# Softmax reciprocals in a windowed attention: spread over a head's 64 partitions by a trip through DRAM instead of by TensorE

## The chip, the cores and the metric

The kernel runs on one core of a Trainium2 chip. The metric is the time of one execution on the device in microseconds (us). Three runs of the kernel before gave 1763.22, 1763.94 and 2857.5 us; their median, 1763.94 us, is what a change is measured against. One more execution was profiled, and the rows of the profile come from that one.

## What is computed

Two layers act on a latent stream of 1024 tokens and a context prefix of 256 tokens, both 1024 wide. Layer 0 is the gated, windowed, grouped-query attention that this document is about; layer 1 is a bidirectional state-space mixer that takes most of the time and is not touched. The part of the reference that matters here:

```python
def sink_softmax(scores, sink_kg, mask):
    if mask is not None:
        scores = jnp.where(mask, scores, -jnp.inf)
    sink_col = jnp.broadcast_to(sink_kg.astype(jnp.float32)[None, :, :, None, None],
                                scores.shape[:-1] + (1,))
    p = jax.nn.softmax(jnp.concatenate([scores, sink_col], axis=-1), axis=-1)
    return p[..., :-1]
...
        s = jnp.einsum('bqkgd,bskd->bkgqs', qb, kb).astype(jnp.float32) * scale
...
        p = sink_softmax(s, sink_kg, mask).astype(vb.dtype)
        return jnp.einsum('bkgqs,bskd->bqkgd', p, vb)
...
    y_lat = ((o * jax.nn.silu(g)) @ w_out).astype(h_lat.dtype)
```

There are 16 query heads of 64 dimensions, 4 to each of 4 key heads. Latent queries, in blocks of 128, see at most three neighbouring blocks of keys and the two blocks of the context; context queries see the two blocks of the context alone.

## The kernel before, in words

**Units.** The attention runs over 40 units, each a block `b` of 128 queries and a key head `j` with its four query heads. Units 1 to 8 are the two context blocks (two key blocks each), units 9 to 24 the first four latent blocks, units 25 to 40 the last four (four or five key blocks each). A unit has a front and a back. `attention` calls the front of unit x+1 and then the back of unit x (`AHEAD=1`).

**Front (`att_front`, lines 747 to 792).** GpSimd starts the loads of the queries (`qs` at line 757, `qz` at 762), SyncE the load of the gate `sg` (758, tag `sgt`, two buffers). For each of the four heads TensorE forms the scores with queries on the partitions (776, 777), VectorE adds the mask and takes the negative row maximum `nm` (781), ScalarE takes the exponential and accumulates the row sum (783). Then, for the four heads at once: GpSimd adds the sink (786), ScalarE takes its exponential (787), GpSimd adds it to the sums (788), and VectorE takes the reciprocal `sums` (790), 128 queries by 4 heads. GpSimd copies it out to `rs` (791), each value repeated 64 times: 128 queries by 2 by 2 by 64, in one buffer.

**Back (`att_back`, lines 794 to 825).** For each key block TensorE turns the four heads' exponentials (802) into a bank of PSUM named `pt` (two buffers), ScalarE and VectorE split them into a high and a low part (806, 807), and TensorE multiplies both with the values (808, 809) into `pv`, which then holds a head's 64 dimensions on partitions and queries along the row. The sums, though, have queries on partitions. So TensorE turns `rs` with two more transposes into `pt` (815): out come 128 partitions, 64 for each of two heads, with a query's reciprocal in every one of them. VectorE multiplies the gate by them (816). ScalarE copies the lower half of `pv` (818), VectorE adds the two halves (821), GpSimd multiplies the result `ot` with the gate (822), and ScalarE and GpSimd split that for the output projection (824, 825).

**Work beside it.** Between key blocks `tick` issues steps of matrix multiplications that have nothing to do with the unit: projections of queries and gates of the second latent half beside units 1 to 24, output projections beside units 25 to 40 (lines 240 to 242). Their weights come through SyncE (233), are split on ScalarE (223) and GpSimd (225), and are asked for one projection ahead. SyncE also loads and stores the residual stream (863, 868, 893) and stores projected queries and gates (663, 664, 672).

**Order.** The program gives dependencies and priorities, and a scheduler puts each engine's instructions in one fixed order by its own model of time. On the chip each engine, and each queue that starts transfers, then runs its own list in order, waiting on semaphores: what stands behind a waiting instruction waits too. SyncE's list holds nearly all the transfers; GpSimd's list holds its arithmetic and the loads of `qs` and `qz`.

Of the kernel before, what the change touches and what calls it, by code (L numbers as in the profile page):

```python
# [9 lines left out]
F32 = mybir.dt.float32  # L10
# [7 lines left out]
P = 128  # L18
# [11 lines left out]
HD = 64  # L30
# [12 lines left out]
    pj=1, S=2, pt=2, pv=1,  # L43
    rope_b=2, qf=3, qh=3, ql=2, kHH=2, kLL=2, qs=2, sgt=2, sm=8, mx=2, nm=2, es=2, sums=2, ph=2, pl=2, co=1, ot=2,
    oraw=3, h1=3, h1k=8, wada=6, gq=1, sqa=1,
    cacc=2, cctx=1, bT=2, cT=2, xn4=4, xn2=1, bn4=4, bn2=1, sz=2, xw=2, hf=2, hx=2, M=2, bw=2, y2=1, xs=1, uT=2, pj2=2, psX=3, sk=2, dg=2,
)
G0 = 4
AHEAD = 1
# [65 lines left out]
class Kernel:  # L115
# [13 lines left out]
    def t(self, pool, shape, dt, tag, bufs=None):  # L129
        self.n += 1  # L130
        kw = {"bufs": bufs or BUFS.get(tag, 1)}
        return pool.tile(shape, dt, tag=tag, name=f"{tag}_{self.n}", **kw)
# [616 lines left out]
    def att_front(self, p, x, i, j, b):  # L749
        nc, t = self.nc, self.t  # L750
        ps = self.psA
        o = b * P - TT[i][0]
        sg = t(self.psm, [P, 2, P], F32, "sgt")
        nm = t(p, [P, R], F32, "nm")
        sums = t(p, [P, R], F32, "sums")
        qs = t(p, [P, R, P], F32R, "qs")
        nc.gpsimd.dma_start(qs, self.q_d[j][i][:, :, :, o : o + P].rearrange("e s d n -> (s d) e n"))
        nc.sync.dma_start(sg, self.sg_d[j][i][:, :, o : o + P].rearrange("e p n -> p e n"))

        z = j % 2  # L760
        qz = self.qz[z]
        nc.gpsimd.dma_start(qz[z * HD : (z + 1) * HD], self.q_d[j][i][:, z, :, o : o + P].rearrange("e d n -> d e n"))
        if b < 8:
            k0, k1 = max(b - 1, 0), min(b + 2, 8)
        else:
            k0, k1 = 8, 8
        kb = list(range(k0, k1)) + [8, 9]
        c0_ = 512 - (k1 - k0) * P
        m0 = {0: 128, 7: 640}.get(b, 0 if b < 8 else 384)
        W = len(kb) * P  # L770
        sms = []
        for r in range(R):
            S = t(self.psS, [P, 1024], F32, "S")
            for x, (qq, kk) in enumerate(((qs[:, r, :], self.kHH[j]), (qz[:, r, :], self.kL[j // 2]))):
                if k1 > k0:
                    nc.tensor.matmul(S[:, c0_:512], qq, kk[:, k0 * P : k1 * P], start=x == 0, stop=x == 1)  # L776
                scored = nc.tensor.matmul(S[:, 512:768], qq, kk[:, LAT : LAT + CTX], start=x == 0, stop=x == 1)  # L777
            self.scored.append(scored.ins)
            Sv = S[:, c0_:768]
            sm = t(self.psm, [P, 640], F32, "sm")  # L780
            nc.vector.tensor_tensor_reduce(out=sm[:, :W], in0=Sv, in1=self.mask[:, m0 : m0 + W], scale=-SCALE, scalar=self.nsink[:, 4 * j + r : 4 * j + r + 1],  # L781
                                           op0=ALU.add, op1=ALU.min, accum_out=nm[:, r : r + 1])
            nc.scalar.activation(sm[:, :W], sm[:, :W], AF.Exp, bias=nm[:, r : r + 1], scale=-1.0, accum_out=sums[:, r : r + 1])  # L783
            sms.append(sm)
        es = t(p, [P, R], F32, "es")
        nc.gpsimd.tensor_tensor(es, nm, self.sink[:, 4 * j : 4 * j + 4], op=ALU.add)
        nc.scalar.activation(es, es, AF.Exp)
        nc.gpsimd.tensor_tensor(sums, sums, es, op=ALU.add)
        rs = t(self.pb, [P, 2, 2, HD], F32, "rs")
        nc.vector.reciprocal(sums, sums)  # L790
        nc.gpsimd.tensor_copy(rs, sums.rearrange("p (x e) -> p e x", e=2).unsqueeze(3).broadcast_to([P, 2, 2, HD]))
        return j, b, i, o, kb, sms, sg, rs

    def att_back(self, p, st, oH, oL, tick):
        nc, t = self.nc, self.t
        ps = self.psA
        j, b, i, o, kb, sms, sg, rs = st
        pv = t(ps, [P, 512], F32, "pv")
        for x, bb in enumerate(kb):
            pt = t(ps, [P, R, P], F32, "pt")  # L800
            for r in range(R):
                nc.tensor.transpose(pt[:, r, :], sms[r][:, x * P : (x + 1) * P], self.ident)  # L802
            ph = t(self.pb, [P, R * P], F32R, "ph")
            pl = t(self.pb, [P, R * P], F32R, "pl")
            ptf = pt.rearrange("p r n -> p (r n)")
            nc.scalar.copy(ph, ptf)  # L806
            nc.vector.tensor_sub(pl, ptf, ph)  # L807
            nc.tensor.matmul(pv, self.v[:, bb, j, :], ph, start=x == 0, stop=False)  # L808
            mm = nc.tensor.matmul(pv, self.v[:, bb, j, :], pl, start=False, stop=x == len(kb) - 1)  # L809
            self.last.append(mm.ins)  # L810
            tick()

        pt = t(ps, [P, 512], F32, "pt")
        for e in range(2):
            nc.tensor.transpose(pt[:, e * P : (e + 1) * P], rs[:, e].rearrange("p x d -> p (x d)"), self.ident)
        nc.vector.tensor_mul(sg, sg, pt[:, : 2 * P].rearrange("p (a n) -> p a n", a=2))
        co = t(self.pb, [HD, 512], F32, "co")
        nc.scalar.copy(co, pv[HD:, :])
        ot = t(self.pb, [P, 2, P], F32, "ot")
        for e in range(2):  # L820
            nc.vector.tensor_add(ot[e * HD : (e + 1) * HD].rearrange("p a n -> p (a n)"), pv[:HD, e * 256 : (e + 1) * 256], co[:, e * 256 : (e + 1) * 256])
        nc.gpsimd.tensor_tensor(ot, ot, sg, op=ALU.mult)
        oh = oH[i][:, 2 * j : 2 * j + 2, o : o + P]
        nc.scalar.copy(oh, ot)
        nc.gpsimd.tensor_tensor(oL[i][:, 2 * j : 2 * j + 2, o : o + P], ot, oh, op=ALU.subtract)  # L825
# [1039 lines left out]
```

## Time and profile before

| what | value |
|---|---|
| runs | 1763.22, 1763.94, 2857.5 us, median 1763.94 |
| the profiled execution | 1765.51 us, of which 1763.5 us from first to last instruction |
| granted TensorE clock in it | 0.997 |
| attention's units, from the first reciprocal to the last turning of `rs` | 254.8 to 681.8 us |
| TensorE turnings of `rs` (line 815) | 80, two for each unit |
| GpSimd copies to `rs` (line 791) | 40 |

In the rows below, PE is TensorE's matrix multiplication and PEld its load of the stationary operand, which runs beside it; DVE is VectorE, ACT ScalarE, POOL GpSimd and SP SyncE. A row such as "PE L815 MATMUL pt<-ident,rs" names the engine, the line, the operation, what is written and what is read; "x80" counts instructions. Three numbers with slashes are the least, middle and greatest duration in ns. "A <- B: 33.1, 20, 3.2" says that A's engine sat idle before A until B was done, for 33.1 us in 20 cases, 3.2 us at most. For a DMA the last number is the median from its start to its landing. Matrix multiplications are pipelined, so that one row's duration overlaps the next row's; the distance from one start to the next says what one occupies.

### The profile page before, as it was taken

The page shows a single profiled execution, that of the slowest core. Times are in us where ns is not written, and L with a number is a line of the kernel's source. Part 1 is how long each engine was busy: PE and PEld are TensorE (multiplying, and loading weights), DVE is VectorE, ACT ScalarE, POOL GpSimd, SP SyncE. Part 2 cuts the span into 40 slices and gives each one's busy share as a digit, 9 for nine tenths or more (in the row PEclk, how much of TensorE's full clock was granted, in tenths as well). Part 3 has the DMA queues.
Part 4 walks back from the last instruction along what each step waited for, and adds up shares of the span by engine and source line. Part 5 has one row for each costly group of instructions (what it writes and reads, how often), then busy time and mean ns, then how long its engine had stood idle before and what let it go on. Part 6 is the DMA issues. An engine that isn't in the chain of part 4 may idle for free.

```text
span 1763.5 us, 28925 instructions
## 1 busy us (share of the span) xinstructions
PE 1731.7 (98%) x10277; PEld 1498.1 (85%) x10277; DVE 1195.1 (68%) x2115; ACT 872.8 (49%) x1905; POOL 794.1 (45%) x1064
## 2 busy tenths in 40 slices
PE   8999999999999998999999999999999999999997
PEld 6897788888888786889898998989889898988886
DVE  5744436788877876685876867677685867876734
ACT  4522247777777774363544434344443444544522
POOL 3231037555565555104454554636455363554311
PEclk9999999999999999999999999999999999999999
DMA  9468876444564436222223232332332332555533
GB/s 364 169 190 261 277 190 146 102 110 96 118 161 130 120 101 219 75 66 68 77 78 97 73 93 70 87 79 75 91 82 76 89 81 79 179 169 172 176 96 131
DMA packets 211389, 225.52 MB, mean 128 GB/s; under 512 B 15789, under 2 KB 149037, under 8 KB 211245
## 3 DMA queue, kind: packets, MB, share of 16 engines
q1 hardware_dynamic: 177180, 205.02, 38.7%
q0 software_dynamic: 34064, 18.65, 5.9%
q8 instruction: 81, 1.33, 0.3%
q14 instruction: 64, 0.52, 0.1%
HBM read 188.78 MB, written 35.13 MB: 127 GB/s over the span
## 4 chain that ended last, share of the span: by engine, by line
PE 88%; DVE 5%; DMA 3%; issue 2%; ACT 1%; POOL 1%; SPq 0%; DVEq 0%; POOLq 0%; ACTq 0%
PE pj L1243 19%; PE pj L1277 10%; PE pj L1682 7%; PE pj L240 7%; PE pj L242 6%; PE pj L241 6%; PE psD L1227 4%; PE pt L802 3%; PE psX L1430 3%; PE psD L1346 2%; PE pv L809 2%; PE pv L808 2%; PE S L776 2%; PE S L777 2%; PE psX L1399 2%
## 5 line engine op out<-in xcount | busy, mean ns | idle before, releaser
L240 PE MATMUL pj<-uH,wh 128*128 128x512 f32 (+1 forms) x632 | 234.3, 371 | 4.9 <-ACT wh L223 1.7
L242 PE MATMUL pj<-uH,wl 128*128 128x512 f32 (+1 forms) x632 | 222.5, 352 | 1.1 <-POOL wl L225 1.1
L241 PE MATMUL pj<-uL,wh 128*128 128x512 f32 (+1 forms) x632 | 222.2, 352 | 0.4 <-POOL uL L825 0.4
L1321 POOL TENSOR_TENSOR xw<-xn,dtdec 128x256 f32<-128x256 f32 x144 | 95.5, 664 | 212.2 <-PE psD L1346 73.4
L1243 PE MATMUL pj<-uH,wh 128*128 128x512 f32 x512 | 173.3, 410 | 0.0
L1243 PE MATMUL pj<-uH,wl 128*128 128x512 f32 x512 | 170.4, 403 | 0.0
L1243 PE MATMUL pj<-uL,wh 128*128 128x512 f32 x512 | 168.8, 403 | 0.0
L1277 PE MATMUL pj<-wl,uH 128*128 128x256 f32 x512 | 151.0, 295 | 0.0
L1277 PE MATMUL pj<-wh,uH 128*128 128x256 f32 x512 | 150.4, 294 | 0.0
L1277 PE MATMUL pj<-wh,uL 128*128 128x256 f32 x512 | 150.0, 293 | 0.0
L807 DVE TENSOR_TENSOR pl<-pt,ph 128x512 fp32r<-128x512 f32 x168 | 115.0, 689 | 47.5 <-ACT ph L806 46.0
L240 PEld LDWEIGHTS pj<-uH,wh 128*128 128x128 f32 x632 | 119.8, 190 | 23.9 <-issue 3.6
L242 PEld LDWEIGHTS pj<-uH,wl 128*128 128x128 f32 x632 | 119.6, 189 | 20.0 <-POOL wl L225 1.6
L781 DVE CUSTOM_DVE_ANT_0 sm<-S,mask,nsink 128x640 f32<-128x640 f32 (+2 forms) x160 | 119.0, 774 | 24.0 <-PE S L777 18.2
L225 POOL TENSOR_TENSOR wl<-wr,wh 128x512 fp32r<-128x512 f32 x74 | 97.1, 1316 | 79.2 <-ACT wh L223 75.8
L1462 ACT ACTIVATE uT<-psX,nw 128x128 f32<-128x128 f32 x128 | 46.5, 363 | 171.8 <-PE psX L1461 167.7
L241 PEld LDWEIGHTS pj<-uL,wh 128*128 128x128 f32 x632 | 120.0, 190 | 12.3 <-issue 0.8
L783 ACT ACTIVATE sm<-sm,nm 128x640 f32<-128x640 f32 (+2 forms) x160 | 118.5, 743 | 21.5 <-DVE nm L781 20.7
L806 ACT CAST ph<-pt 128x512 fp32r<-128x512 f32 x168 | 97.9, 584 | 48.7 <-PE pt L802 45.5
L223 ACT CAST wh<-wr 128x512 fp32r<-128x512 f32 (+1 forms) x116 | 74.8, 648 | 84.6 <-PE pj L241 59.7
L1243 PEld LDWEIGHTS pj<-uH,wl 128*128 128x128 f32 x512 | 95.9, 188 | 19.9
L1243 PEld LDWEIGHTS pj<-uL,wh 128*128 128x128 f32 x512 | 95.3, 188 | 19.1
(357 smaller groups left out, 4933.0 us busy)
## 6 DMA issues: line engine op xcount, KB each, us to landing
wr<-w_x SPq DMA_DIRECT2D x32, 512.0 KB, 4.2
M<-acs SPq DMA_DIRECT2D x64, 256.0 KB, 5.0
bw<-acs SPq DMA_DIRECT2D x64, 256.0 KB, 5.4
wr<-w_sk SPq DMA_DIRECT2D x24, 512.0 KB, 3.9
wr<-wg SPq DMA_DIRECT2D x40, 256.0 KB, 5.2
qs<-q POOLq DMA_DIRECT2D x40, 256.0 KB, 3.9
wada<-w_ada SPq DMA_DIRECT2D x16, 512.0 KB, 8.0
wr<-wq SPq DMA_DIRECT2D x32, 256.0 KB, 3.4
```

The lines of the kernel that those rows point to most:

```text
L225: (eng or nc.vector).tensor_tensor(l, raw, h, op=ALU.subtract)
L240: self.nc.tensor.matmul(ps, lh, rh, start=first and i == 0, stop=False)
L241: self.nc.tensor.matmul(ps, lh, rl, start=False, stop=False)
L242: self.last_mm = self.nc.tensor.matmul(ps, ll, rh, start=False, stop=last and i == n - 1)
L781: nc.vector.tensor_tensor_reduce(out=sm[:, :W], in0=Sv, in1=self.mask[:, m0 : m0 + W], scale=-SCALE, scalar=self.nsink[:, 4 * j + r : 4 * ...
L783: nc.scalar.activation(sm[:, :W], sm[:, :W], AF.Exp, bias=nm[:, r : r + 1], scale=-1.0, accum_out=sums[:, r : r + 1])
L806: nc.scalar.copy(ph, ptf)
L807: nc.vector.tensor_sub(pl, ptf, ph)
L1243: self.pe = nc.tensor.matmul(raw[:, 512 * i : 512 * i + 512], l[:, k, :], r[i][:, k, :], start=k + y == 0, stop=k == KT - 1 and y == 2)
L1277: self.pe = nc.tensor.matmul(pj[:, c], l, r[:, k, :], start=c % 2 + q + k + y == 0, stop=c % 2 == 1 and q == 1 and k == 3 and y == 2)
L1321: nc.gpsimd.tensor_tensor(xw, X(st, c).rearrange("p (r h) -> p r h", r=R), self.dtdec[:, c, hd(d, g)].unsqueeze(2).broadcast_to([P, R, HP] ...
L1682: self.pe = nc.tensor.matmul(banks[x], l[:, z, sl], r, start=k == 2 * qs[0] and y == 0, stop=k == 2 * qs[-1] + 1 and y == 2)
```

## The change

The reciprocals no longer go through GpSimd and TensorE. At the end of the front SyncE stores `sums` to DRAM, turned around on the way, so that a head's 128 reciprocals lie in a row; the tensor there is a separate one for each unit. At the start of the back SyncE loads them in two transfers, one for each half of the partitions, and reads each row 64 times over, so that the reciprocals arrive as line 816 needs them. The SBUF tile `rs` now has two buffers, each as large as the old one. The two transposes, their use of a `pt` bank and the GpSimd copy are gone; VectorE's multiplication reads SBUF where it read PSUM.

```diff
-        rs = t(self.pb, [P, 2, 2, HD], F32, "rs")
         nc.vector.reciprocal(sums, sums)
-        nc.gpsimd.tensor_copy(rs, sums.rearrange("p (x e) -> p e x", e=2).unsqueeze(3).broadcast_to([P, 2, 2, HD]))
+        rs = t(self.dr, [2, 2, P], F32, f"rs{j}_{b}")
+        nc.sync.dma_start(rs.rearrange("x e q -> q (x e)"), sums)
         return j, b, i, o, kb, sms, sg, rs
...
         pv = t(ps, [P, 512], F32, "pv")
+        rb = t(self.pb, [P, 2, P], F32, "rs")
+        for x in range(2):
+            nc.sync.dma_start(rb[x * HD : (x + 1) * HD], rs[x].unsqueeze(0).broadcast_to([HD, 2, P]))
...
-        pt = t(ps, [P, 512], F32, "pt")
-        for e in range(2):
-            nc.tensor.transpose(pt[:, e * P : (e + 1) * P], rs[:, e].rearrange("p x d -> p (x d)"), self.ident)
-        nc.vector.tensor_mul(sg, sg, pt[:, : 2 * P].rearrange("p (a n) -> p a n", a=2))
+        nc.vector.tensor_mul(sg, sg, rb)
```

The table of buffer counts gets one more entry, `rs=2`.

More of the change, by code (lines that the diff above doesn't have):

```diff
@@ L45 @@
     oraw=3, h1=3, h1k=8, wada=6, gq=1, sqa=1,
-    cacc=2, cctx=1, bT=2, cT=2, xn4=4, xn2=1, bn4=4, bn2=1, sz=2, xw=2, hf=2, hx=2, M=2, bw=2, y2=1, xs=1, uT=2, pj2=2, psX=3, sk=2, dg=2,
+    cacc=2, cctx=1, bT=2, cT=2, xn4=4, xn2=1, bn4=4, bn2=1, sz=2, xw=2, hf=2, hx=2, M=2, bw=2, y2=1, xs=1, uT=2, pj2=2, psX=3, sk=2, dg=2, rs=2,
 )
```

## The prediction, on record before the result

> **What bounds the kernel now.** I read the page's busy times and its chain first, then the stages of the attention, then who waits for whom in them.
>
> ```profile
> span 1763.5 us, 28925 instructions
> PE 1731.7 (98%) x10277; PEld 1498.1 (85%) x10277; DVE 1195.1 (68%) x2115; ACT 872.8 (49%) x1905; POOL 794.1 (45%) x1064
> ...
> PE 88%; DVE 5%; DMA 3%; issue 2%; ACT 1%; POOL 1%; SPq 0%; DVEq 0%; POOLq 0%; ACTq 0%
> ```
>
> TensorE is busy 98% of the span and makes 88% of the chain that ended last; GpSimd makes 1% of it. The change touches only the attention, so I look at its stages (columns: busy us of PE, PEld, DVE, ACT, POOL, then the granted clock, the DMA share and GB/s).
>
> ```profile
> 254.00:300.00 46.00, 44.97 (x247) 37.44 (x248) 30.86 (x99) 34.79 (x101) 32.69 (x54) 1.00 0.66 147
> 300.00:480.00 180.00, 177.39 (x1032) 151.41 (x1031) 145.40 (x319) 132.77 (x297) 101.64 (x152) 1.00 0.48 111
> 480.00:545.00 65.00, 62.68 (x447) 57.20 (x446) 47.70 (x101) 49.22 (x107) 44.48 (x59) 1.00 0.58 153
> 545.00:662.00 117.00, 114.43 (x650) 94.61 (x649) 90.56 (x192) 84.04 (x189) 60.81 (x88) 1.00 0.43 112
> ```
>
> In each stage TensorE has 96 to 99%; VectorE comes next (145.40 of 180, 81%), GpSimd is at 52 to 71%. So TensorE's own work is what a change here is worth, and the other engines matter through the stalls that they give it. Those are, from 250 to 690 us, with the two waits around the removed instructions:
>
> ```profile
> POOL rs L791 <- PE pt L815: 33.1, 20, 3.2
> DVE sgt L816 <- PE pt L815: 5.1, 5, 1.5
> PEld pv L809 <- DVE pl L807: 11.3, 25, 1.0
> PEld pj L241 <- POOL uL L825: 0.8, 1, 0.8
> PEld S L242 <- POOL wl L225: 0.6, 1, 0.6
> ```
>
> GpSimd stands 33.1 us until an earlier unit's turnings free the single `rs`, but TensorE loses only 0.8 and 0.6 us to GpSimd's products. The long wait is on an engine with time to spare.
>
> **What is removed.** The three groups:
>
> ```profile
> L815 PE MATMUL pt<-ident,rs x80: 270/272/328, 259.0 to 681.9; 128*128 128x128 f32 x80
> L791 POOL COPY rs<-sums x40: 389/397/627, 256.4 to 662.3; 128x256 f32<-128x256 f32 x40
> L816 DVE TENSOR_TENSOR sgt<-sgt,pt x40: 407/414/422, 259.5 to 682.3; 128x256 f32<-128x256 f32 x40
> ```
>
> 80 times 272 ns would be 21.8 us, but matmuls overlap, so I take what a pair occupies from the starts of its neighbours:
>
> ```profile
> 414.35 0.40 PE L809 MATMUL pv<-pl,v 128*128 128x512 f32 x1
> 414.58 0.38 PE L815 MATMUL pt<-ident,rs 128*128 128x128 f32 x2
> 414.72 0.49 PE L240 MATMUL pj<-uH,wh 128*128 128x512 f32 x1
> 415.04 0.39 PE L241 MATMUL pj<-uL,wh 128*128 128x512 f32 x1
> ```
>
> A 512-column multiplication occupies 0.23 us (414.35 to 414.58). From the pair's start to L241 it is 0.46 us, and one 512-column multiplication is in that, so the pair takes 0.46 - 0.23 = 0.23 us. Forty pairs: **-9.2 us**, all in a stream that is nearly full. The Trainium skill's page "TensorE: Matmul & The Clock Gate", section "Part 4: PE-mode transpose", gives about 275 ns for one 128x128 transpose inside a kernel. This trace agrees in the duration (272 ns), but by it as a price the removal would be 22 us and the time about 1744; the spacing of the rows, 115 ns each, decides.
>
> GpSimd loses 40 x 0.4 = 16 us of copies and the 33.1 us of waiting. I cost this at nothing: the cover is GpSimd's idle third, and without that cover it could be worth the 1.4 us (0.8 + 0.6) that TensorE waits for it. A unit also no longer takes a `pt` bank out of turn; VectorE's 5.1 us of waiting for L815 go. They reach TensorE only if VectorE was the last to arrive, so their bounds are 0 and -5.1; I take 0, because TensorE's waits for VectorE come before L809 and not behind L816. The multiplication itself stays at 0.41 us: its output is as large as before.
>
> **What is added.** For each unit SyncE gets three transfers: a store of 2 KB that, by its access pattern, goes element by element (128 x 4, no two neighbours in DRAM), and two loads of 64 rows of 1 KB. Nothing in the trace is such a store. The nearest are:
>
> ```profile
> k<-qh SPq DMA_DIRECT2D x4, 256.0 KB, 2.0
> q<-qh SPq DMA_DIRECT2D x14, 128.0 KB, 2.4
> sgt<-sg SPq DMA_DIRECT2D x17, 128.0 KB, 2.3
> 787.36 1.67 SPq L1076 DMA_DIRECT2D eald<-tot  x2
> 794.32 0.34 SPq L1077 DMA_DIRECT2D eal<-eald  x1
> ```
>
> From below: whole-row stores land in 2.0 to 2.4 us and the gate's load in 2.3; with 0.2 for the reciprocal and 0.4 for the first of two load issues the chain from a reciprocal's start to its arrival is 0.2 + 2.4 + 0.4 + 2.3 = 5.3 us. From above: layer 1 has the same trick once, a store of pieces of 20 bytes (L1076), read back spread (L1077). There the load could start only 794.32 - 787.36 = 7.0 us after the first store. So the chain is 0.2 + 7.0 + 0.4 + 2.3 = 9.9 us. In kind the change is nearest to this row; but two stores stand in it, with other loads behind them, so I take a chain nearer 6 us and keep both ends.
>
> What covers this is the gap between the reciprocal and the multiplication at line 816, one unit later:
>
> ```profile
> 254.83 0.17 DVE L790 RECIPROCAL sums<-sums 128x4 f32<-128x4 f32 x1
> 259.50 0.41 DVE L816 TENSOR_TENSOR sgt<-sgt,pt 128x256 f32<-128x256 f32 x1
> 279.16 0.17 DVE L790 RECIPROCAL sums<-sums 128x4 f32<-128x4 f32 x1
> 282.16 0.42 DVE L816 TENSOR_TENSOR sgt<-sgt,pt 128x256 f32<-128x256 f32 x1
> 301.03 0.17 DVE L790 RECIPROCAL sums<-sums 128x4 f32<-128x4 f32 x1
> 308.34 0.42 DVE L816 TENSOR_TENSOR sgt<-sgt,pt 128x256 f32<-128x256 f32 x1
> 409.36 0.18 DVE L790 RECIPROCAL sums<-sums 128x4 f32<-128x4 f32 x1
> 427.08 0.41 DVE L816 TENSOR_TENSOR sgt<-sgt,pt 128x256 f32<-128x256 f32 x1
> ```
>
> The first pair is unit 1, the second unit 4, the third unit 8, the last unit 19. In the eight context units the gaps are 4.7, 6.5, 7.1, 3.0, 6.9, 7.3, 5.0 and 7.3 us; unit 9 has 8.1, unit 10 10.9, and from unit 13 on it is 15 us and more. So a chain of 6 us is late in units 1, 4 and 7, by 1.3 + 3.0 + 1.0 = 5.3 us together; at 9.9 us it is late in units 1 to 9, by 33 us together. A late arrival stops VectorE's list at line 816; behind it stand the next masks (781) and low parts (807), which TensorE needs. TensorE has projections to run meanwhile, so I take half of 5.3: **+2.5 us**. If the whole is hidden it is 0, if all of the 33 us comes through it is +33.
>
> **SyncE's list** grows by 120 issues of about 0.4 us and by a wait of one store's landing before each pair of loads. Behind that stand weights (233), gates (758), residuals (863, 893). SyncE waits most of the stage already:
>
> ```profile
> SPq L758 <- POOL ot L822: 81.8, 25, 7.0
> SPq L233 <- POOL wl L225: 51.9, 28, 6.5
> SPq L233 <- POOL rs L791: 31.5, 8, 6.1
> ```
>
> These are waits for free buffers, in which the new issues fit, and weights are asked for a projection ahead. I cost the list at 0; if its waits come at a bad time, see the rivals. **DMA engines:** the stage from 300 to 480 us moves
>
> ```profile
> DMA packets 24623, 19.99 MB, mean 111 GB/s; under 512 B 1712, under 2 KB 19359, under 8 KB 24607
> ```
>
> at a share of 0.48, which is 0.48 x 16 x 180 / 24623 = 0.056 us a packet. A unit adds at most 512 + 128 = 640 packets (an estimate from the access patterns), 36 us of packet time, or 2.2 us on each of 16 engines in a unit of some 11 us: the share rises by about 0.2 and stays under 0.7. No price.
>
> **Sum.** -9.2 + 2.5 = -6.7 us in the profiled execution: 1765.5 becomes 1758.8. The median of the runs is 1.6 us below that execution, so **1757 us**, 0.4% less. About 2%, some 35 us, is what a measurement of this kernel can tell from no change; the forecast is inside.
>
> **Rivals.**
>
> *More gain, 1747 us.* Beside the -9.2 us VectorE's 5.1, GpSimd's 1.4 and a tenth of the 11.3 us that TensorE waits for low parts go: -16.8. For it: GpSimd's list no longer stops at `rs`. Against it: none of these waits is TensorE's at that place.
>
> *Nothing, 1764 us.* The 0.23 us of a unit go into waits for the next exponential, since VectorE and ScalarE feed TensorE all along (the 11.3 us). Against it: TensorE is fuller than either.
>
> *Late reciprocals, 1788 us, the one that ends on the slower side.* The element-wise store is slow, and VectorE stops in the context units, each in its list at line 816: -9.2 + 33 = +24. It decides as soon as the chain exceeds 7.3 us, the widest of the eight gaps; above 15 us, or if the scheduler puts the multiplication early in VectorE's list because it thinks the load short, the units from 10 on pay as well, and at 1 us for each of those 31 the time passes 1800. For it: the 7.0 us of L1077. Against it: GpSimd's multiplication at 822 has more room than line 816. The Trainium skill's page "DMA: Bandwidth & Descriptors", section "Rules for kernel authors", says that a strided last dimension becomes one descriptor for each element, and warns against turning data by a rearranged access pattern. By that rule this store is the slow kind; no row of this trace shows one of 512 single elements.
>
> *SyncE in the way, 1773 us.* A load waits for a store's landing while residuals or weights for the output projections stand behind it. If each of the 16 projections of units 25 to 40 is late by 1 us: -6.7 + 16 = +9. For it: the fullest stage of SyncE is the one from 480 us. Against it: in that stretch TensorE's only wait for a weight product is the 0.6 us above.
>
> **How the numbers follow.** Forecast 0.48 (its own range 1751 to 1762), more gain 0.12, nothing 0.15, late reciprocals 0.17, SyncE 0.08. The low end, 1744, is the more-gain case with a further 3 us from the low parts; the high end, 1789, takes in late reciprocals at their price. Beyond lie half of that rival (0.08) and a little of the others (0.05). Over 2% faster would need 35 us, nearly four times what the transposes occupy: 0.02. Over 2% slower is the upper half of late reciprocals and a bad tail of SyncE: 0.09. Within 2%: 0.89.
>
> **What would show it.** Right: no rows of 815 and 791; GpSimd busy 16 us less; TensorE busy about 9 us less between 254 and 682 us; line 816 at 0.41 us with waits for a DMA only in context units, under 6 us in all; layer 1 as long as before. Wrong: a store whose dependent load starts 5 us or more after it, a wait of VectorE for a DMA at line 816 in latent units, or TensorE waiting for residuals or weights between 480 and 690 us.

## The result and the profile after

The changed kernel takes 2096.7 us (median of 5 runs, 2092 to 2099) beside 1763.2 us for the kernel before: a ratio of 1.189, with a 95% interval of 1.188 to 1.191. It is 333 us slower, where 1757 us had been forecast in a range of 1744 to 1789.

The page of the changed kernel, busy times and then the chain that ended last:

```profile
span 2096.3 us, 28932 instructions
PE 1803.3 (86%) x10197; PEld 1556.2 (74%) x10197; DVE 1193.3 (57%) x2115; ACT 875.7 (42%) x1905; POOL 778.8 (37%) x1024
...
PE 53%; DMA 12%; DVE 2%; issue 2%; ACT 1%; POOL 1%; SPq 1%; DVEq 0%; POOLq 0%; ACTq 0%
PE pj L1243 16%; PE pj L1277 9%; DMA rs<-sums 8%; PE pj L1682 6%; PE psD L1227 3%; DMA rs<-rs 3%; PE psX L1430 3%; PE psD L1346 2%; PE pj L240 1%; PE psX L1399 1%; PE psX L1398 1%; PE pj L241 1%; PE pj L242 1%; PE psX L1405 1%; DMA h<-h 1%
```

The 80 transposes and the 40 copies are gone as planned (10277 to 10197 on PE, 1064 to 1024 on POOL). But TensorE has fallen from 98% to 86%, and two transfers that did not exist before stand in the chain: the store of the reciprocals (rs<-sums, 8%) and their load (rs<-rs, 3%). The stages say where the time went. The kernel before, split at the end of its attention (columns: the stage, its length, then busy us of PE, PEld, DVE, ACT, POOL, the granted clock, the DMA share and GB/s):

```profile
254.00:682.00 428.00, 418.35 (x2462) 355.70 (x2462) 320.61 (x719) 309.05 (x707) 250.53 (x362) 1.00 0.51 127
682.00:1764.00 1082.00, 1066.52 (x6291) 941.34 (x6289) 749.39 (x1172) 477.51 (x1031) 477.34 (x631) 1.00 0.35 101
```

The changed kernel in the same two parts:

```profile
254.00:1001.00 747.00, 473.65 (x2307) 399.80 (x2305) 315.34 (x709) 306.76 (x697) 228.22 (x314) 0.79 0.39 75
1001.00:2096.00 1095.00, 1082.86 (x6363) 955.60 (x6363) 752.89 (x1182) 482.39 (x1042) 484.26 (x639) 0.99 0.36 103
```

The attention takes 747 us in place of 428; the rest is 13 us longer. TensorE has 63% of that stage. Who waited for whom in it:

```profile
DVE sgt L816 <- DMA rs<-rs: 284.3, 36, 12.5
ACT sm L783 <- DVE nm L781: 152.9, 37, 10.8
...
PE S L776 <- DVE nm L781: 76.6, 15, 10.1
...
PE pt L805 <- DVE pl L810: 74.1, 12, 11.1
...
PE pv L812 <- DVE pl L810: 46.6, 9, 10.4
...
ACT sm L783 <- DMA rs<-sums: 37.6, 5, 9.8
```

VectorE stands 284 us at the multiplication of line 816, in 36 of 40 units, and TensorE and ScalarE stand for what VectorE has behind it in its list. One wait is of another kind: ScalarE cannot write new row sums until the store has read the old ones (37.6 us). SyncE's own list:

```profile
SPq L801 <- DMA rs<-sums: 320.5, 40, 10.7
```

SyncE stands 320 us before the loads, in each of the 40 units. One such place, on SyncE (the store of a unit, then nothing until its loads):

```profile
408.28 0.37 SPq L791 DMA_DIRECT2D rs<-sums  x1
417.94 1.09 SPq L801 DMA_DIRECT2D rs<-rs  x2
419.12 0.54 SPq L791 DMA_DIRECT2D rs<-sums  x1
```

And on VectorE at the same time:

```profile
408.09 0.16 DVE L789 RECIPROCAL sums<-sums 128x4 f32<-128x4 f32 x1
...
411.46 0.18 DVE L789 RECIPROCAL sums<-sums 128x4 f32<-128x4 f32 x1 [1.29 <-POOL sums L788]
413.01 0.69 DVE L810 TENSOR_TENSOR pl<-pt,ph 128x512 fp32r<-128x512 f32 x1 [1.38 <-ACT ph L809]
421.35 0.42 DVE L816 TENSOR_TENSOR sgt<-sgt,rs 128x256 f32<-128x256 f32 x1 [7.65 <-DMA rs<-rs]
```

The reciprocal is there at 408.1, the store starts at 408.3 and has landed at about 417.9, the loads land at about 421.3. In VectorE's list only five computing instructions stand between this reciprocal and its multiplication (the short reads of the row maximum left out), so VectorE stands 7.65 us. It is so everywhere: in the units from 9 on the median is 6 such instructions, where it was 21 in the kernel before. Finally the transfers, from 300 to 1000 us (the last number is the median from start to landing):

```profile
qs<-q POOLq DMA_DIRECT2D x34, 256.0 KB, 6.1
...
rs<-rs SPq DMA_DIRECT2D x74, 64.0 KB, 3.3
sgt<-sg SPq DMA_DIRECT2D x35, 128.0 KB, 2.5
...
rs<-sums SPq DMA_DIRECT2D x37, 2.0 KB, 9.1
```

A store of 2 KB takes 9 us, longer than a load of 256 KB. And the queries' loads, which have nothing to do with the change, land in 6.1 us where they took 3.9.

### The profile page after: what moved, and what is told of

Read it like the earlier page. It is cut to its first block, busy times and chain, and to the rows that moved or that the text cites. A ratio compares the mean times of both kernels' runs of the same rounds, so it can differ in the third digit from the quotient of the medians.

```text
span 2096.3 us, 28932 instructions
## 1 busy us (share of the span) xinstructions
PE 1803.3 (86%) x10197; PEld 1556.2 (74%) x10197; DVE 1193.3 (57%) x2115; ACT 875.7 (42%) x1905; POOL 778.8 (37%) x1024
## 4 chain that ended last, share of the span: by engine, by line
PE 53%; DMA 12%; DVE 2%; issue 2%; ACT 1%; POOL 1%; SPq 1%; DVEq 0%; POOLq 0%; ACTq 0%
PE pj L1243 16%; PE pj L1277 9%; DMA rs<-sums 8%; PE pj L1682 6%; PE psD L1227 3%; DMA rs<-rs 3%; PE psX L1430 3%; PE psD L1346 2%; PE pj L240 1%; PE psX L1399 1%; PE psX L1398 1%; PE pj L241 1%; PE pj L242 1%; PE psX L1405 1%; DMA h<-h 1%
## 5 line engine op out<-in xcount | busy, mean ns | idle before, releaser
L240 PE MATMUL pj<-uH,wh 128*128 128x512 f32 (+1 forms) x632 | 244.2, 386 | 21.2 <-DVE h L867 12.5
L241 PE MATMUL pj<-uL,wh 128*128 128x512 f32 (+1 forms) x632 | 231.9, 367 | 0.0
L242 PE MATMUL pj<-uH,wl 128*128 128x512 f32 (+1 forms) x632 | 230.4, 365 | 0.0
L805 PE MATMUL pt<-ident,sm 128*128 128x128 f32 x672 | 119.9, 305 | 83.9 <-DVE pl L810 83.8
L816 DVE TENSOR_TENSOR sgt<-sgt,rs 128x256 f32<-128x256 f32 x40 | 19.3, 481 | 288.5 <-DMA rs<-rs 284.3
L805 PEld LDWEIGHTS pt<-ident,sm 128*128 128x128 f32 x672 | 95.3, 158 | 107.3 <-DVE pl L810 79.5
L240 PEld LDWEIGHTS pj<-uH,wh 128*128 128x128 f32 x632 | 127.4, 202 | 42.4 <-DVE h L867 13.6
L242 PEld LDWEIGHTS pj<-uH,wl 128*128 128x128 f32 x632 | 126.5, 200 | 20.6 <-DVE wl L225 1.3
L241 PEld LDWEIGHTS pj<-uL,wh 128*128 128x128 f32 x632 | 127.7, 202 | 14.2 <-issue 0.8
L776 PE MATMUL S<-kHH,qs 128*128 128x384 f32 (+1 forms) x128 | 55.5, 434 | 82.0 <-DVE nm L781 76.6
```

The lines of the kernel that those rows point to most:

```text
L240: self.nc.tensor.matmul(ps, lh, rh, start=first and i == 0, stop=False)
L241: self.nc.tensor.matmul(ps, lh, rl, start=False, stop=False)
L242: self.last_mm = self.nc.tensor.matmul(ps, ll, rh, start=False, stop=last and i == n - 1)
```

## The experiments

Three theories were at hand. A: the store is slow by the number of its pieces, and VectorE waits for it. B: the multiplication's place in VectorE's list is what costs; a unit later even a slow store would be covered. C: SyncE, standing before the loads, holds back weights and residuals. A fourth, D, came after the second group of runs below: the store also holds up transfers that have nothing to do with it. The kernel before, timed beside each run, took 1761 to 1763 us.

**Fewer, larger pieces.** Two kernels differ from the change in the store alone:

```diff
-        nc.sync.dma_start(rs.rearrange("x e q -> q (x e)"), sums)
+        nc.sync.dma_start(rs.rearrange("x e q -> x (e q)").rearrange("x (q c) -> q x c", c=2), sums.rearrange("q (x c) -> q x c", c=2))
```

> The store of the reciprocals goes in 256 pieces of 8 bytes in place of 512 of 4; loads, instruction counts and the planned order stay nearly the same. The reciprocals land in another order in DRAM, so the gates get other queries' reciprocals. Theory A (the store is slow by its pieces: 9.0 us for 512, some 2.2 us for whole rows, so about 13 ns a piece): it lands in 5.6 us, VectorE's wait at the multiplication falls by 3.4 us a unit, and the time falls from 2097 to about 1960 us. Rival (the store's 9 us are a fixed price of a transfer of this kind, whatever the pieces): 9 us again and 2097.

```diff
-        nc.sync.dma_start(rs.rearrange("x e q -> q (x e)"), sums)
+        nc.sync.dma_start(rs.rearrange("x e q -> (x e q)").rearrange("(q c) -> q c", c=R), sums)
```

> The store goes in 128 pieces of 16 bytes, one for each partition; again the order in DRAM is another, so the gates get other queries' reciprocals. Theory A: it lands in 3.9 us, VectorE's wait falls by 5.1 us a unit, the time is about 1890 us. Rival (fixed price): 9 us and 2097.

Measured: 1888.5 us (ratio 1.071) and 1808.3 us (ratio 1.026, interval 1.023 to 1.029). The store lands in a median of 4.1 us with 8-byte pieces and 2.4 us with 16-byte pieces; VectorE's wait for the loads falls from 284 to 122 and 57 us. The fixed price is out. But a constant price for each piece does not fit either: from 512 to 256 pieces 4.9 us go (19 ns for each piece saved), from 256 to 128 only 1.7 (13 ns), and both kernels are 70 to 80 us faster than theory A said. Even at 2.4 us the two-step trip still costs 47 us.

**The multiplication later.**

```diff
-        nc.vector.tensor_mul(sg, sg, rb)
...
-            nc.vector.tensor_add(ot[e * HD : (e + 1) * HD]...
+            add = nc.vector.tensor_add(ot[e * HD : (e + 1) * HD]...
+        with self.tc.issue_after(add.ins):
+            nc.vector.tensor_mul(sg, sg, rb)
```

> The change with VectorE's multiplication of the gate moved behind the unit's two additions (issued after the second of them); store and loads as in the change. Theory B (the place in VectorE's list decides: the multiplication stands a few us behind the reciprocal, and a unit later the 13 us of store and load would be covered): under 1850 us, and VectorE's wait for the loads under 80 us of the 284. Rival C (SyncE, which stands 320 us behind the stores, is what holds the rest back): still above 1950 us, with waits for weights or gates in place of those at the multiplication.

Measured: 1974.7 us (ratio 1.120). VectorE's wait for the loads fell to 30.5 us, as theory B wanted, but only 122 of the 333 us came back. What stood in its place, from 254 to 900 us:

```profile
ACT sm L783 <- DMA rs<-sums: 73.5, 14, 10.0
POOL ot L823 <- DVE sgt L822: 59.9, 24, 9.6
...
ACT wh L223 <- DMA wr<-wo: 44.5, 8, 10.2
DVE h L301 <- DMA h<-h: 43.7, 6, 12.2
```

ScalarE waits for the store to release the sums and for weights (wr), VectorE for the residual (h). SyncE stood 354 us before the loads. That spoke for C, so the next kernels took away these waits one after the other.

**More buffers, then loads further back.** Four buffers for the sums on top of the late multiplication:

```diff
-es=2, sums=2, ph=2,
+es=2, sums=4, ph=2,
```

> The multiplication behind the additions as in the run before it, and four buffers in place of two for the row sums, so that ScalarE's next sums need not wait until the slow store has read the old ones. If that wait (73.5 us there) is a cost of its own: about 1975 - 70 = 1905 us, and SyncE's 354 us behind the stores, with weights and residuals late by them, keeps the rest. If ScalarE's wait was only time that it would have stood elsewhere: 1965 to 1975 us.

Measured: 1972.4 us (ratio 1.120). That is two us less, no more than the runs of one kernel differ (1972.5 and 1976.9 without the buffers): ScalarE's 73.5 us were time that it would have stood elsewhere, and VectorE's wait for the loads rose from 30.5 to 73.5 us.

Then the loads behind the next unit's gate in SyncE's list, with the late multiplication and without it:

```diff
-        nc.sync.dma_start(sg, self.sg_d[j][i][:, :, o : o + P]...
+        self.gload = nc.sync.dma_start(sg, self.sg_d[j][i][:, :, o : o + P]...
...
         for x in range(2):
-            nc.sync.dma_start(rb[x * HD : (x + 1) * HD], ...
+            with self.tc.issue_after(self.gload.ins):
+                nc.sync.dma_start(rb[x * HD : (x + 1) * HD], ...
```

> As the run before, and the two loads of a unit stand in SyncE's list behind the load of the next unit's gate, so that the slow store has landed before SyncE comes to them. Result as the reference's. If the three waits (VectorE at the multiplication, ScalarE for the sums, SyncE for the store) are the whole loss: SyncE's wait for the stores under 60 us and the time between 1752 and 1775 us. If the store's 512 pieces also hold up other transfers on the DMA engines: above 1790 us, with the queries' loads still landing in 6 us in place of 3.9.

> The change with four buffers for the sums and the loads behind the next unit's gate load, but the multiplication free for the scheduler to place. If the place of the loads in SyncE's list is the main thing, since it moves the multiplication back by itself: within 15 us of the run before it. If the scheduler still sets the multiplication ahead of the loads' landing: 1800 us and more, with VectorE waiting for the loads.

Measured: 1927.3 us (ratio 1.094, interval 1.092 to 1.096) with the late multiplication, 2015.5 us (ratio 1.144) without it. In the first SyncE's wait for the stores fell from 357 to 61 us, and still 166 us were lost; so C is a part and not the whole. VectorE still waited 88 us for the loads there, in 22 places, so this kernel did not take away all the waits either. In the second the scheduler set the multiplication ahead of the loads' landing, and VectorE waited 223 us. In both the queries' loads took 8 us to land.

**The removal alone, and the store alone.** One kernel is the kernel before without any spreading: no copy, no transposes, no DRAM, the gate multiplied by a tile of ones, so that the softmax sums are left out of the result.

```diff
-        rs = t(self.pb, [P, 2, 2, HD], F32, "rs")
         nc.vector.reciprocal(sums, sums)
-        nc.gpsimd.tensor_copy(rs, ...)
...
-        pt = t(ps, [P, 512], F32, "pt")
-        for e in range(2):
-            nc.tensor.transpose(pt[:, e * P : (e + 1) * P], ...)
-        nc.vector.tensor_mul(sg, sg, pt...)
+        nc.vector.tensor_mul(sg, sg, self.ones.unsqueeze(1).broadcast_to([P, 2, P]))
```

> The kernel before without the copy on GpSimd, the two transposes and DRAM; VectorE multiplies the gate by a tile of ones, so the softmax sums are left out of the result. It shows what the removal alone is worth. The forecast's price (0.23 us for a pair of transposes, nothing for GpSimd's wait): 1763 - 9 = 1754 us. By the transposes' full duration (272 ns each): 1741 us. If GpSimd's 33 us of waiting mattered: under 1735 us. If other waits take the place: 1763.

Measured: 1752.7 us beside 1761.7 (ratio 0.994, interval 0.993 to 0.996): 8.9 us less. The multiplication needs neither transposes nor reciprocal here, and in the units from 9 on a median of one instruction stands between it and the reciprocal, where it was 21: without the transposes nothing keeps it late in VectorE's list.

The other is the kernel before, transposes and all, with one store added for each unit that nothing waits for, and four buffers for the sums:

```diff
         nc.gpsimd.tensor_copy(rs, ...)
+        rd = t(self.dr, [2, 2, P], F32, f"rd{j}_{b}")
+        nc.sync.dma_start(rd.rearrange("x e q -> q (x e)"), sums)
         return j, b, i, o, kb, sms, sg, rs
```

> The kernel before with one thing added: each unit also stores its reciprocals to DRAM in 512 pieces, as the change does, but nobody loads them (and four buffers for the sums, so that nobody waits for the store). It prices the store's traffic alone. If the loss is waiting alone: 1762 to 1772 us, though the store lands in 9 us. If the pieces hold up the other transfers: 1790 us and more.

Measured: 1875.9 us (ratio 1.064, interval 1.062 to 1.066). A store of 2 KB that nobody reads costs 114 us in 40 units, 2.9 us each. This is the run that shows theory D. Its stage from 300 to 480 us, and the queries' loads in the whole run's attention, 254 to 800 us:

```profile
300.00:480.00 180.00, 162.72 (x901) 136.54 (x900) 125.01 (x284) 116.39 (x268) 90.71 (x136) 0.95 0.94 100
```

```profile
qs<-q POOLq DMA_DIRECT2D x37, 256.0 KB, 8.4
```

The DMA engines are busy 0.94 of the stage, where they had 0.48, and move fewer GB/s (100 for 111). The queries land in 8.4 us in place of 3.9. In those 180 us their queue has 12800 packets (the parts that a transfer is moved in) for 41.7% of the engines' time, 94 ns each; before it had 13600 for 21.4%, 45 ns each. All packets of 4 bytes, the store's pieces among them, take only 226 of the 2693 us that the engines are busy in the stage. So their time goes to the other transfers' packets, which are held up. The waits from 254 to 800 us say the same: VectorE stood 30.4 us for residuals (before 4.7), ScalarE 20.9 us for weights of the output projections (`wr<-wo`), and TensorE's multiplications 30 us for queries; neither of these last two waits is in the list of before.

**How far apart the pieces lie.** The same store for nobody, with only the pieces changed: first 16 bytes in a piece, then 4 bytes in a piece with 512, 64 and 16 bytes from one to the next. All have four buffers for the sums.

```diff
+        rd = t(self.dr, [P, R], F32, f"rd{j}_{b}")
+        nc.sync.dma_start(rd, sums)
```

> The kernel before with a store of each unit's reciprocals that nobody loads, in 128 pieces of 16 bytes in place of 512 of 4 (which cost 114 us). If the price goes with the pieces: a quarter or less, 1762 to 1790 us. If it is any extra transfer in SyncE's list: 1850 us and more.

```diff
+        rd = t(self.dr, [2, 2, P, P], F32, f"rd{j}_{b}")
+        nc.sync.dma_start(rd.rearrange("x e q c -> q (x e) c")[:, :, 0:1], sums.unsqueeze(2))
```

> The kernel before with a store that nobody loads, in 512 pieces of 4 bytes, each 512 bytes from the next in DRAM, so that no two are neighbours there. If the price is one for each piece: about 1875 us, as with neighbouring pieces, and a landing of about 9 us. If it comes from many small writes into the same few hundred bytes: under 1800 us and a landing under 5 us.

The last two have 16 and 4 elements in place of 128 as the last dimension of rd:

> The kernel before with a store that nobody loads, 512 pieces of 4 bytes, each 64 bytes from the next. 512 bytes apart cost nothing (1760 us, landing 2.1 us), 4 bytes apart cost 114 us. If what counts is a stretch of DRAM of more than 64 bytes that several pieces share: above 1775 us and a landing above 3 us. If 64 bytes are far enough: 1758 to 1768 us.

> The same with the pieces 16 bytes apart. If pieces that share 64 bytes hold each other up, four of them here: between, 1770 to 1830 us and a landing of 3 to 6 us. If the price comes only from pieces that touch each other: 1758 to 1768 us.

| store that nobody reads, 2 KB | landing, median | us | ratio (interval) |
|---|---|---|---|
| 512 pieces of 4 bytes, 4 bytes apart | not recorded; 9.0 in the change | 1875.9 | 1.064 (1.062 to 1.066) |
| 512 pieces of 4 bytes, 16 bytes apart | 2.9 | 1765.6 | 1.001 (1.000 to 1.003) |
| 512 pieces of 4 bytes, 64 bytes apart | 2.3 | 1760.9 | 0.999 (0.998 to 1.000) |
| 512 pieces of 4 bytes, 512 bytes apart | 2.1 | 1760.4 | 0.999 (0.998 to 0.999) |
| 128 pieces of 16 bytes, touching | 2.1 | 1765.2 | 1.001 (1.000 to 1.002) |

The same stage with the pieces 512 bytes apart, and its transfers:

```profile
300.00:480.00 180.00, 177.12 (x1034) 151.00 (x1033) 145.78 (x319) 132.62 (x295) 101.90 (x150) 1.00 0.50 109
```

```profile
qs<-q POOLq DMA_DIRECT2D x36, 256.0 KB, 4.0
...
rd<-sums SPq DMA_DIRECT2D x39, 2.0 KB, 2.0
```

512 pieces of 4 bytes cost nothing when they lie apart: the DMA share is 0.50, the store lands in 2 us, the queries in 4.0. So it is not their number. Nor is it touching as such: 128 pieces of 16 bytes touch, and land in 2.1 us. What goes with the landing is how many pieces share a short stretch of DRAM: sixteen in 64 bytes land in 9.0 us, eight in 4.1 (the change with 8-byte pieces), four in 2.1 to 2.9, one in 2.3. The 64 bytes are only a measure to compare by; no run found where such a stretch begins or ends, and with four in it the time is already that of the kernel before. Theory A, in the form of a price for each piece, has fallen; theory D holds, with its cause in the addresses. That the writes into one short stretch wait for each other inside the memory or the DMA engine is an argument from this table; no run looked inside.

**The change with its pieces apart.** The two DRAM tensors are filled once beforehand, and the loads read one row of 512 bytes for each head.

```diff
-        rs = t(self.dr, [2, 2, P], F32, f"rs{j}_{b}")
-        nc.sync.dma_start(rs.rearrange("x e q -> q (x e)"), sums)
+        rs = self.rsd[len(self.scored) // R % 2]
+        nc.sync.dma_start(rs.rearrange("x e q c -> q (x e) c")[:, :, 0:1], sums.unsqueeze(2))
...
-            nc.sync.dma_start(rb[x * HD : (x + 1) * HD], rs[x].unsqueeze(0).broadcast_to([HD, 2, P]))
+            nc.sync.dma_start(rb[x * HD : (x + 1) * HD], rs[x][:, 0].unsqueeze(0).broadcast_to([HD, 2, P]))
```

> The change as it is, except that its 512 pieces of 4 bytes land 512 bytes apart in DRAM (in two tensors used in turn, filled beforehand), and the loads read one whole row of 512 bytes for each head, of which one element is a reciprocal: the gates get other numbers. If neighbouring pieces are the root: the store lands in some 2.1 us, as where nobody loaded it, and the time is that of the 16-byte pieces, 1795 to 1825 us. If 512 pieces are slow once somebody waits for them: 2000 us and more.

Measured: 1837.2 us (ratio 1.041, interval 1.034 to 1.048), a little above what was expected. The store lands in 2.5 us. What is left, from the list of waits and from SyncE's:

```profile
DVE sgt L819 <- DMA rs<-rsd: 68.6, 32, 5.5
```

```profile
SPq L804 <- DMA rsd<-sums: 56.8, 36, 2.8
```

So with a quick store 75 of the 333 us remain: the trip of two transfers, in lists that leave no room for it (in the units from 9 on the median distance from reciprocal to multiplication is again 6 instructions). Here the loads also take 3.7 us, in place of 2.9 with the 16-byte pieces; each partition's row comes in two parts here, but whether that is why was not tried.

**Both cures together.** First the 16-byte store, with late multiplication, four sums buffers and loads behind the next gate:

```diff
-        nc.sync.dma_start(rs.rearrange("x e q -> q (x e)"), sums)
+        nc.sync.dma_start(rs.rearrange("x e q -> (x e q)").rearrange("(q c) -> q c", c=R), sums)
```

> The run with late multiplication, four sums buffers and loads behind the next gate load, with the store in 128 pieces of 16 bytes in place of 512 (the gates get other queries' reciprocals). If the 512 pieces are the root of what was left there (1927 us) and the three waits the rest: 1752 to 1762 us, at best the 1753 of the kernel without any spreading. If going through DRAM costs by itself: 1775 us and more.

Measured: 1753.8 us (ratio 0.994, interval 0.993 to 0.996). That is the kernel without spreading (1752.7) within its spread: the trip through DRAM can be hidden whole. Its gates hold other queries' reciprocals, though. The last kernel computes the right ones: beside the same late multiplication, buffers and loads, VectorE turns the sums in blocks of 32 by 32, in one of two tiles (`wide`) that are filled once at the start:

```diff
-        nc.vector.reciprocal(sums, sums)
+        w = self.wide[len(self.scored) // R % 2]
+        nc.vector.reciprocal(w[:, :R], sums)
+        tr = t(p, [P, 32], F32, "tr", 4)
+        nc.vector.transpose(tr, w)
...
-        nc.sync.dma_start(rs.rearrange("x e q -> q (x e)"), sums)
+        for c in range(4):
+            nc.sync.dma_start(rs.rearrange("x e q -> (x e) q")[:, 32 * c : 32 * c + 32], tr[32 * c : 32 * c + R])
```

> Result as the reference's: VectorE turns the sums itself in blocks of 32 by 32 (one more instruction a unit), four stores of four rows of 128 bytes replace the store of 512 pieces, and loads and multiplication stand late as before. If few pieces and a late place are all that it takes: the transposes' 9 us are won, less what VectorE's turning costs, 1752 to 1760 us, so faster than the kernel before by a little. If four more issues on SyncE or the turning on VectorE cost more than 9 us: 1765 us and more.

Measured: 1751.7 us (ratio 0.993, interval 0.992 to 0.994): 11.4 us faster than the kernel before, and 345 us faster than the change. The new instruction, the remaining wait and the stage:

```profile
L792 DVE STREAM_TRANSPOSE tr<-wide x40: 197/208/214, 253.3 to 647.6; 128x32 f32<-128x32 f32 x40
```

```profile
DVE sgt L827 <- DMA rs<-rs: 4.5, 2, 3.1
```

```profile
300.00:480.00 180.00, 175.40 (x1010) 150.58 (x1011) 152.82 (x344) 133.77 (x299) 99.11 (x136) 0.99 0.52 124
```

Forty turnings of 208 ns are 8.3 us on VectorE, which has 152.82 of 180 us in the stage; the wait for the loads is 4.5 us in all.

## Why the prediction was wrong, point by point

Three steps of the sum failed. The chain from reciprocal to arrival was taken at 6 us and was about 13. The cover was read from the old list, 15 us and more in the latent units, and was gone in the new one. The DMA engines were given "no price", and the store's traffic by itself cost 114 us. No one of them is the whole: by the forecast's own cover even a chain of 9.9 us gave only 1788 us. Two of the signs that it named for being wrong were there: the loads started 9.7 us after the store, and VectorE waited at line 816 in the latent units.

**What bounds the kernel, and what the removal is worth: right.** The forecast priced the pair of transposes at 0.23 us, 9.2 us in all, and GpSimd's copies and 33 us of waiting at nothing. The kernel without spreading measured 8.9 us for all of these together. The price by the transposes' full duration, 22 us, was the wrong one. (That VectorE comes next after TensorE holds in two of the four stages only; in the other two ScalarE is fuller, with 34.79 of 46 and 49.22 of 65 us. Nothing in the sum rests on it.)

**The chain from reciprocal to arrival: too short, and its upper bound was no bound.** The forecast held 5.3 to 9.9 us and took 6. In the change the store lands in 9.0 us and the loads in 3.3; the unit shown above took 421.35 - 408.09 = 13.3 us. The bound came from a store of 20-byte pieces; the table shows that larger pieces and wider spacing lie on the quick side, so that row bounded from below. The Trainium skill's rule that a strided last dimension becomes one descriptor for each element ("DMA: Bandwidth & Descriptors", section "Rules for kernel authors") gave the right warning and not the price: the same 512 elements land in 9.0 us when neighbours in DRAM and in 2.1 us when 512 bytes apart.

**The cover: read from the wrong list.** The forecast took the gap between the reciprocal and line 816 in the old order, 15 us and more in latent units. But that gap was made by the transposes that the change removes. With them gone the scheduler set the multiplication a median of 6 instructions behind the reciprocal in those units, in place of 21; without the loads too, in the kernel without spreading, it is 1. The forecast had this as an aside in its rival "late reciprocals", at 1 us for each latent unit. It was 7.9 us in 36 units (284.3 / 36). The late multiplication brought back 122 us.

**"SyncE's list: I cost the list at 0": wrong.** SyncE stood 320 us. The rival "SyncE in the way" had the mechanism, at 1 us in 16 places. It is not the whole either: freed of most of that wait (61 us were left), with buffers and a late multiplication, the kernel still lost 166 us.

**"DMA engines: no price": wrong, and the largest cost measured by itself.** The forecast counted packets at the mean price of the old stage, 0.056 us, for a share of under 0.7. Its count of 512 for a store was right: the store that nobody reads added 8723 packets under 512 bytes in the stage, 513 for each of 17 stores. But the price did not hold: that stage has 0.94 x 16 x 180 / 31444 = 0.086 us a packet, because the other transfers' packets take longer beside such a store, and 114 us of time went. With the pieces 512 bytes apart the stage has more packets still, 33730, at a share of 0.50. The forecast's "no two neighbours in DRAM" is true only of the order in which the access pattern names the elements; the 512 pieces fill 2 KB without a gap, and that is what mattered. No row of the trace before shows such a store, as the forecast itself says of it, so the range had to allow for one.

**Where the 333 us went.** Traffic of the slow store with nobody waiting: 114 us. Waits with a quick store: 75 us (pieces apart) or 47 us (16-byte pieces). Together that leaves 144 to 172 us, which have no run of their own. That they come from the two together, since each wait is as long as the store is slow, is an argument and was not shown. A wait that nobody had forecast, ScalarE's for the row sums, was worth no more than the spread of the runs when it was taken away beside the others.

## What to carry to other kernels

A gap between two instructions in an old list covers nothing once the instruction that made it is gone: for each new wait, ask where the scheduler will put the waiting instruction, and put it late by hand. Before data go to DRAM turned around, look at the addresses of the pieces: here 4-byte pieces side by side slowed the transfers that were under way beside them, and the same pieces further apart did not. A transfer's price has two parts, the time until it lands and what it does to the others; a kernel that issues it and never waits measures the second.

## What the runs showed of the hardware

- A store of 512 touching 4-byte pieces took 9.0 us to land, 256 touching 8-byte pieces 4.1, 128 touching 16-byte pieces 2.1 to 2.4; 512 4-byte pieces took 2.9, 2.3 and 2.1 us at 16, 64 and 512 bytes from each other.
- Beside the slow stores that nobody waited for, loads started from another queue, GpSimd's, landed in 8.4 us in place of 3.9, and their packets took 94 ns in place of 45.
- TensorE's granted clock fell with its idle time: 1.00 in the attention before, 0.79 after, and there it was busy 474 us with fewer instructions than it had in 418 us before. So part of the loss is the price of waiting itself: of the 319 us that the attention grew, TensorE's idle time is 264 and its busy time 55. The Trainium skill ("TensorE: Matmul & The Clock Gate", section "HAM oscillation — how this bites in real kernels") says that a wait for a DMA that lasts long enough between matmuls lets the clock fall back, so that the next ones start slow; the trace agrees, and in the kernels whose waits are gone the clock of the whole execution is back at 0.997, where the change has 0.921.
- VectorE turned a 128 by 32 tile of four-byte elements, block by block, in 208 ns.
